# The first feed-forward product of a two-layer encoder: one matmul for high and low tokens in four of seven products

## The chip, the core and the metric

The kernel runs on one NeuronCore of a Trainium2 chip. The metric is the time of one execution on the device, in microseconds (us); several runs are made and their median is given.

TensorE (PE in the profile) multiplies and writes its sums to PSUM, a memory of eight banks with 512 columns of 32 bits each. VectorE (DVE) and ScalarE (ACT) work on elements in SBUF and PSUM. GpSimd (POOL) here mainly issues transfers that add to what lies at their target; SyncE (SP) issues plain transfers. Each engine goes through its own queue in order and waits for the others by semaphores.

## What is computed

Two layers, 512 tokens of width 1024. Each layer has attention of two kinds, and then the feed-forward part that this change touches:

```python
h = rmsnorm(x, mlp_norm[l])
u = jnp.square(jax.nn.relu(jnp.einsum('bsd,df->bsf', h, w_ff1[l])))
x = x + jnp.einsum('bsf,fd->bsd', u, w_ff2[l])
```

`w_ff1` is 1024 x 4096, `w_ff2` 4096 x 1024. All is float32.

## The kernel before, in words

**Precision by parts.** Each factor is split into a high part (rounded to the matmul's own format, fp32r) and a low part (what is left). A product a·b is then three matmuls: high·high, high·low, low·high (`three`, L295). Weights come by DMA as float32 tiles of 128 x 1024 and are split on their way: ScalarE makes the high part `whi` (L131), VectorE the low part `wlo` (L132).

**Seven products for eight.** Both feed-forward products use a Strassen-Winograd scheme: the operands are cut into 2 x 2 blocks, and seven products of sums of blocks replace eight. For the first product, the sums of token blocks lie in `T_hi`, `T_lo` (`opening`, L884, makes them, number 0 to 3), the plain tokens in `h_hi`, `h_lo`. The sums of weights are made on the fly. With W11, W12, W21, W22 as the four blocks, the tile called y holds W11, z holds W12, x holds W21 and has W22 added by a second transfer on GpSimd's queue (L852), w holds W22.

**Groups and units.** A layer's 4096 columns go in 4 groups (g = 0 to 3). In a group come the 14 units of the first product (seven products q in the order of `HALVES` L50, each for two halves c of the columns), then the seven forms of the second product (`FORMS` L43: 11, 21, x1, 22, x2, x3, x4), with 24 matmuls of 512 columns each. A unit (q,c) has 24 matmuls of 256 columns: two blocks of columns i, four steps cc along the width, three matmuls each (L1121 to L1124). Its moving operand is a block of 256 tokens (`MOVES`, L945), its stationary one a piece of the weights.

**What happens with the sums.** Products share PSUM banks: bank a takes product 1, then 6, 7 and 4 on top of it; bank c takes 2; bank b takes 5 and then 3. In between `tap` (L960) reads the running sums: product 1's sum is copied to F1 by ScalarE (L970), 2 is added to F1 by VectorE (L972); after 6 the sum is copied to F0 (L975); after 7 to F2 (L977) with bank b added (L978); after 3 bank b is added to F0 (L983); after 4 the sum goes straight from PSUM. Each of F0 to F3 is then bent: ReLU and square, two passes of ScalarE (L967). Some combinations of F0 to F4 follow on VectorE (`behind_3`, L999; `behind_4`, L1007), and `roll` splits an F into high and low parts `Ah`, `Al` for the second product (L245).

**What sets the order.** The order on each engine is that in which the program issues, kept by `line` (L267), which chains all splits, taps, bends, rolls and gathers on ScalarE and on VectorE. When a unit is issued, `W.next` (L162) first issues the weight splits up to four units ahead (`do_split`, L147); then the deferred bends and rolls of the unit before (`come_to`), then the unit's matmuls, then its tap. There are five pairs of tiles for split weights, so the split four units ahead can only run when the unit before the current one is done. So at unit (1,0) of a group, the splits up to the fifth unit of `HALVES` stand ahead of the tap of (1,0), on both engines.

**Hooks.** `then` (L907 ff.) hangs work behind a split: behind the split of 5, `sum1` "y" (L862) adds W11 to x on VectorE, giving product 6's weights, and has W21 added to y by a GpSimd transfer (L864), giving product 7's; behind the split of 6 (in the first group of 7), `sum1` "z" adds W12, giving product 3's. The tiles for the next group are loaded behind splits of the second product: x behind those of form x4. `paced` makes such a load wait for the last split. The first group's tiles are loaded during attention.

```python
def do_split(self, n, ahead=None):
    while self.split < min(n, self.stop):
        ...
        self.split_part(i, 0, 1024)
        ...
        for fn in self.then.pop(i, ()):
            fn()
```

## Time and profile before

| | us |
|---|---|
| median of 3 runs | 1120.12 (1119.45 to 1121.89) |
| the profiled execution | 1119.62 |
| its span in the profile | 1117.8 |
| first product, one group (third group of the first layer, 398.33 to 438.64) | 40.31 |
| second product, one group (438.64 to 476.75) | 38.11 |
| in the first of these, busy: VectorE, ScalarE | 31.71, 26.49 |

A line of the timeline reads: start in us from the span's start, duration in us, engine, line, operation, `out<-in` by the program's names, shapes, count; in brackets the idle time of the engine before it and what ended it. The tile names `q`, `yw`, `ww` and `cs` stand for raw weights, `f` for the first product's sums. A group's line (`x64 | 24.9, 390`) gives count, busy time in us and mean in ns.

### The profile page before, as it was taken

How to read it: one execution, taken by the hardware profiler on the slowest of the kernel's cores; microseconds unless marked ns; L12 is line 12 of the kernel's file. 1: busy time of each engine (PE TensorE's matmuls, PEld its weight loads, DVE VectorE, ACT ScalarE, POOL GpSimd, SP SyncE). 2: the span in 40 equal slices, each digit the busy share in tenths (PEclk: the TensorE clock that was granted, in tenths of full speed). 3: DMA queues.
4: the chain of work that ended last, by engine and by line, in shares of the span. 5: the costliest groups of instructions: out<-in, count | busy, mean ns of one | idle time of the engine just before them, and what ended most of it. 6: DMA issues, size and time to landing. Idle time of an engine off the chain costs nothing.

```text
span 1117.8 us, 17696 instructions
## 1 busy us (share of the span) xinstructions
PE 1109.3 (99%) x6654; PEld 985.1 (88%) x6654; DVE 929.5 (83%) x1230; ACT 709.5 (63%) x1113; POOL 176.9 (16%) x257
## 2 busy tenths in 40 slices
PE   9999999999999999999999999999999999999997
PEld 7888989889889899899888889888998998998986
DVE  7878789788897877878888787897988888888787
ACT  6546666677767557567555467675777665565675
POOL 1001334210210110201000014440101102011022
PEclk9999999999999999999999999999999999999999
DMA  7746334266887776876537463523578768859665
GB/s 249 208 123 203 114 116 114 81 170 188 186 197 214 167 176 204 189 190 158 123 113 208 119 177 113 157 77 142 105 229 185 189 189 187 206 138 202 172 135 148
DMA packets 60613, 183.37 MB, mean 164 GB/s; under 512 B 7536, under 2 KB 8816, under 8 KB 60528
## 3 DMA queue, kind: packets, MB, share of 16 engines
q1 hardware_dynamic: 46416, 131.62, 37.1%
q0 software_dynamic: 13824, 50.34, 25.7%
q8 instruction: 53, 0.87, 0.3%
q10 hardware_dynamic: 288, 0.28, 0.1%
q14 instruction: 32, 0.26, 0.1%
HBM read 154.95 MB, written 2.10 MB: 140 GB/s over the span
## 4 chain that ended last, share of the span: by engine, by line
PE 85%; DVE 5%; DMA 4%; issue 3%; ACT 2%; POOL 1%; POOLq 0%; DVEq 0%; SPq 0%; ACTq 0%
PE f L300 8%; PE f L298 8%; PE f L299 8%; DMA q<-in_w 3%; PE x L299 2%; PE x L298 2%; PE x L300 2%; PE wo L298 2%; PE wo L299 2%; PE wo L300 2%; DVE wlo L132 1%; DMA st1d1q<-hl1d1k 1%; PE T1s L623 1%; PE T0s L623 1%; PE v0u L298 1%
## 5 line engine op out<-in xcount | busy, mean ns | idle before, releaser
L132 DVE TENSOR_TENSOR wlo<-q,whi 128x1024 fp32r<-128x1024 f32 x184 | 223.6, 1220 | 23.9 <-ACT whi L131 22.6
L131 ACT ACTIVATE whi<-q 128x1024 fp32r<-128x1024 f32 x184 | 191.2, 1052 | 65.3 <-DMA q<-in_w 32.3
L298 PE MATMUL f<-T_hi,whi 128*128 128x256 f32 x512 | 145.5, 284 | 0.0
L300 PE MATMUL f<-T_hi,wlo 128*128 128x256 f32 x512 | 144.9, 283 | 0.0
L299 PE MATMUL f<-T_lo,whi 128*128 128x256 f32 x512 | 144.9, 283 | 0.0
L876 POOL DMA_DIRECT2D q<-in_w x64 | 56.2, 913 | 366.2 <-DVE wlo L132 346.4
L298 PE MATMUL f<-h_hi,whi 128*128 128x256 f32 x384 | 108.8, 283 | 0.0
L299 PE MATMUL f<-h_lo,whi 128*128 128x256 f32 x384 | 108.7, 283 | 0.0
L300 PE MATMUL f<-h_hi,wlo 128*128 128x256 f32 x384 | 108.7, 283 | 0.0
L299 PEld LDWEIGHTS f<-T_lo,whi 128*128 128x128 f32 x512 | 98.3, 192 | 0.0
L298 PEld LDWEIGHTS f<-T_hi,whi 128*128 128x128 f32 x512 | 98.3, 192 | 0.0
L300 PEld LDWEIGHTS f<-T_hi,wlo 128*128 128x128 f32 x512 | 98.2, 192 | 0.0
L967 ACT ACTIVATE F<-F 128x512 f32<-128x512 f32 x112 | 70.4, 629 | 21.7 <-DVE F L972 17.8
L131 ACT ACTIVATE whi<-raw 128x1024 fp32r<-128x1024 f32 (+1 forms) x58 | 55.7, 970 | 31.7 <-PE wo L299 6.9
L298 PEld LDWEIGHTS f<-h_hi,whi 128*128 128x128 f32 x384 | 73.7, 192 | 0.4
L299 PEld LDWEIGHTS f<-h_lo,whi 128*128 128x128 f32 x384 | 73.7, 192 | 0.3
L300 PEld LDWEIGHTS f<-h_hi,wlo 128*128 128x128 f32 x384 | 73.7, 192 | 0.1
L132 DVE TENSOR_TENSOR wlo<-raw,whi 128x1024 fp32r<-128x1024 f32 (+1 forms) x58 | 68.1, 1186 | 5.7 <-ACT whi L131 5.7
L245 ACT ACTIVATE Ahx<-F 128x1024 fp32r<-128x1024 f32 x32 | 34.0, 1061 | 52.1 <-PE x L299 24.4
L245 DVE TENSOR_TENSOR Alx<-F,Ahx 128x1024 fp32r<-128x1024 f32 x32 | 39.2, 1225 | 8.6 <-ACT Ahx L245 8.6
L245 DVE TENSOR_TENSOR Al<-F,Ah 128x1024 fp32r<-128x1024 f32 x24 | 29.4, 1224 | 18.0 <-ACT Ah L245 18.0
L556 POOL TENSOR_TENSOR sig1s<-sig1s,C1s 128x128 f32<-128x128 f32 (+3 forms) x32 | 28.5, 892 | 57.6 <-DVE C1s L553 46.7
(994 smaller groups left out, 3242.0 us busy)
## 6 DMA issues: line engine op xcount, KB each, us to landing
q<-in_w SPq DMA_DIRECT2D x100, 512.0 KB, 5.1
q<-in_w POOLq DMA_DIRECT2D x84, 512.0 KB, 7.0
raw<-in_w SPq DMA_DIRECT2D x62, 512.0 KB, 4.2
yw<-in_w SPq DMA_DIRECT2D x12, 512.0 KB, 4.5
yw<-in_w POOLq DMA_DIRECT2D x12, 512.0 KB, 5.6
cs<-in_w SPq DMA_DIRECT2D x8, 512.0 KB, 7.9
ww<-in_w SPq DMA_DIRECT2D x8, 512.0 KB, 4.0
x<-in_xT SPq DMA_DIRECT2D x8, 256.0 KB, 4.2
```

Of the source, the lines that this page charges most:

```text
L131: h = nc.scalar.activation(hi[:, a:b], raw[:, a:b], AF.Copy)
L132: self.last = h, nc.vector.tensor_tensor(out=lo[:, a:b], in0=raw[:, a:b], in1=hi[:, a:b].bitcast(F32), op=ALU.subtract)
L245: return nc.scalar.activation(hi, src, AF.Copy), nc.vector.tensor_tensor(out=lo, in0=src, in1=hi.bitcast(F32), op=ALU.subtract)
L298: return (nc.tensor.matmul(pt, ah, bh, start=first, stop=False, skip_group_check=onto), nc.tensor.matmul(pt, ah, bl, start=False, stop=Fal ...
L299: nc.tensor.matmul(pt, ah, bl, start=False, stop=False, skip_group_check=onto),
L300: nc.tensor.matmul(pt, al, bh, start=False, stop=last, skip_group_check=onto))
L556: nc.gpsimd.tensor_mul(sig[:, 0:wd], sig[:, 0:wd], C[:, 1 : wd + 1])
L623: nc.tensor.transpose(pt[:, n * P : (n + 1) * P], u["w"][qi][:, kb * P : (kb + 1) * P], ident)
L876: paced(nc.gpsimd.dma_start(t, quad(g, q, c), accum_op=ALU.add))
L967: nc.scalar.activation(o, o if i is None else i, fn, scale=by)))
```

## The change

1. The high and low parts of the tokens come to lie in one tile (`h2`, `T2`). In the products 1, 2, 6 and 4 one matmul of 512 columns takes the high weights against high and low tokens, and writes the two sums side by side: columns 0 to 255 of a bank hold high·high, 256 to 511 high·low. The matmul low·high has 256 columns as before and goes onto the first half. Products 5, 3 and 7 keep their three matmuls.
2. So bank a becomes four banks (0 to 3: two blocks of columns for each c). Sums are forked in PSUM: after product 1, ScalarE copies both banks of a into two others (c, banks 4 to 7), and product 2 accumulates on the copy; after product 6, ScalarE copies the low half of a into a bank b, and 5 and 3 accumulate on it. The taps add high and low halves when they take them, in pieces of 256 columns; after 4 the sum goes through F3 by a copy and an addition.
3. The order of the products becomes 1, 2, 6, 5, 3, 7, 4. Product 6's weights are made by `sum1` "y" ahead of the split of 6 (a new kind of hook, `first`), as W11 + x in the tile y; product 3's by `sum1` "z" in the tile z, behind the split of 6 (first group: behind the one of the next unit).
4. Product 7's weights can no longer be made in the tile y, so W11 is loaded anew and W21 added to it (`fill("7")`), behind the split of 6 and `sum1` "z". The load of form 21 moves behind the split of 5.
5. The roll of form 21 goes in two halves, one for each c; `opening` 1 is issued at (1,1) in place of (2,0), 3 at (7,0). The transposes for the MLP norm's sums move from behind (1,0) to behind (6,1) of the second group.

```diff
-HALVES = ("1", "2", "5", "6", "7", "3", "4")
-LAYS = (("5", 1), ("6", 0), ("6", 1), ("7", 0))
+HALVES = ("1", "2", "6", "5", "3", "7", "4")
+LAYS = (("5", 1), ("3", 0), ("7", 0), ("7", 1))
...
+            self.first.pop(i, lambda: None)()
             self.split_part(i, 0, 1024)
...
-    banks = {"t": 2, "mm": 2, "s": 3, "o": 1}
...
+    def one(k, name):
+        return ps.tile([P, 512], F32, tag=f"k{k}", name=name, bufs=1)
...
-    h_hi = cp.tile([P, KC, S], F32R, tag="h_hi", name="h_hi")
-    h_lo = cp.tile([P, KC, S], F32R, tag="h_lo", name="h_lo")
+    h2 = cp.tile([P, 2, KC, S], F32R, tag="h", name="h")
+    h_hi, h_lo = h2[:, 0, :, :], h2[:, 1, :, :]
...
-            T_hi = fr.tile([P, KC, S], F32R, tag="T_hi", name=f"T_hi{l}")
-            T_lo = fr.tile([P, KC, S], F32R, tag="T_lo", name=f"T_lo{l}")
+            T2 = fr.tile([P, 2, KC, S], F32R, tag="T", name=f"T{l}")
+            T_hi, T_lo = T2[:, 0, :, :], T2[:, 1, :, :]
...
             def fill(what, g, c):
-                t = homes[(what, c)] if what in "yw" else kept["x.z".index(what)][c]
-                for q in {"y": "1", "z": "2", "x": "5", "w": "4"}[what] + {"y": "7", "x": "63"}.get(what, ""):
+                if what == "7":
+                    t = homes["y", c] if g else (F[3], kept[1][0])[c]
+                else:
+                    t = homes[(what, c)] if what in "yw" else kept["x.z".index(what)][c]
+                for q in {"y": "16", "z": "23", "x": "5", "w": "4", "7": "7"}[what]:
                     W.raw[_AT[("q", l, g, q, c)]] = t
-                paced(nc.sync.dma_start(t, quad1(g, {"y": "11", "z": "12", "x": "21", "w": "22"}[what], c)))
-                if what == "x":
-                    nc.gpsimd.dma_start(t, quad1(g, "22", c), accum_op=ALU.add)
+                paced(nc.sync.dma_start(t, quad1(g, {"y": "11", "z": "12", "x": "21", "w": "22", "7": "11"}[what], c)))
+                if what in "x7":
+                    nc.gpsimd.dma_start(t, quad1(g, "22" if what == "x" else "21", c), accum_op=ALU.add)
...
             def sum1(what, g, c):
-                i = _AT[("q", l, g, "5", c)]
-                t, by = W.raw[i], W.raw[_AT[("q", l, g, "1" if what == "y" else "2", c)]]
+                t, by = (W.raw[_AT[("q", l, g, q, c)]] for q in ("65" if what == "y" else "36"))
                 line(v=nc.vector.tensor_add(t, t, by))
-                if what == "y":
-                    nc.gpsimd.dma_start(by, quad1(g, "21", c), accum_op=ALU.add)
...
-                    then("q", g, "5", c, sum1, "y", g, c)
-                    then("q", g, "6" if g else "7", c, sum1, "z", g, c)
-                    then("q", g, "2" if g else "7", c, fetch, g, "21", c)
+                    first("q", g, "6", c, sum1, "y", g, c)
+                    then("q", g, "6" if g or not c else "5", c if g else 1 - c, sum1, "z", g, c)
+                    if g:
+                        then("q", g, "6", c, fill, "7", g, c)
+                        then("q", g, "5", c, fetch, g, "21", c)
+                    else:
+                        then("q", g, "7", 1, fetch, g, "21", c)
+                        if c == 0:
+                            then("q", g, "6", 1, fill, "7", g, 1)
...
+            fill("7", 0, 0)
...
-                a, b = ((h_hi, h_lo), (T_hi, T_lo))[which]
-                return a[:, k + cc, t], b[:, k + cc, t]
+                m = (h2, T2)[which]
+                return m[:, 0, k + cc, t], m[:, 1, k + cc, t], m[:, :, k + cc, t]
...
+            def tap(g, q, c):
+                at = 512 * c
+                halves = [slice(at + 256 * i, at + 256 * i + 256) for i in range(2)]
+
+                def bend(n, scale=1.0):
+                    o = F[n][:, at : at + 512]
+                    for fn, by in ((AF.Relu, scale), (AF.Square, 1.0)):
+                        put_off.append(lambda fn=fn, by=by: line(nc.scalar.activation(o, o, fn, scale=by)))
+
+                def take(n, kind, lows):
+                    for h, t in zip(halves, sums[kind, c]):
+                        line(nc.scalar.copy(F[n][:, h], t[:, 256:512] if lows else t[:, 0:256]))
+
+                def more(n, kind, lows):
+                    for h, t in zip(halves, sums[kind, c]):
+                        line(v=nc.vector.tensor_add(F[n][:, h], F[n][:, h], t[:, 256:512] if lows else t[:, 0:256]))
 
                 if q == "1":
-                    line(nc.scalar.copy(f(1), pt))
+                    sums["c", c] = some((4 + 2 * c, 5 + 2 * c), f"fc{l}{g}{c}")
+                    for to, t in zip(sums["c", c], sums["a", c]):
+                        line(nc.scalar.copy(to, t))
                 elif q == "2":
-                    line(v=nc.vector.tensor_add(f(1), f(1), pt))
+                    take(1, "c", False)
+                    more(1, "c", True)
+                elif q == "6":
+                    take(0, "a", False)
+                    sums["b", c] = one(4 + c, f"fb{l}{g}{c}")
+                    for i, t in enumerate(sums["a", c]):
+                        line(nc.scalar.copy(sums["b", c][:, 256 * i : 256 * i + 256], t[:, 256:512]))
...
                     bend(1)
-                elif q == "6":
-                    line(nc.scalar.copy(f(0), pt))
+                elif q == "5":
+                    line(nc.scalar.copy(F[2][:, at : at + 512], sums["b", c]))
+                elif q == "3":
+                    o = F[0][:, at : at + 512]
+                    line(v=nc.vector.tensor_add(o, o, sums["b", c]))
+                    bend(0)
                 elif q == "7":
-                    line(nc.scalar.copy(f(2), pt))
-                    line(v=nc.vector.tensor_add(f(2), f(2), sums[("b", c)]))
+                    more(2, "a", False)
                     bend(2, -1.0)
                 elif q == "4":
-                    bend(3, -1.0, pt)
-                elif q == "3":
-                    line(v=nc.vector.tensor_add(f(0), f(0), pt))
-                    bend(0)
+                    take(3, "a", True)
+                    more(3, "a", False)
+                    bend(3, -1.0)
...
-                line(*roll("21"))
+                line(*roll("21", 512, 1024))
...
-                        n = {("2", 0): 1, ("5", 0): 2, ("3", 0): 3}.get((q, c))
+                        n = {("1", 1): 1, ("5", 0): 2, ("7", 0): 3}.get((q, c))
...
+                        if (q, c) == ("1", 0):
+                            for c_ in range(GP // 2):
+                                sums["a", c_] = some((2 * c_, 2 * c_ + 1), f"fa{l}{g}{c_}")
...
                         for i in range(2):
+                            joint, onto = q in "1264", q != "1"
+                            to = pt[:, 256 * i : 256 * i + 256] if spot == "b" else pt[i] if joint else pt[i][:, 0:256]
+                            steps = [[] for _ in range(2)]
                             for cc in range(4):
-                                ops = three(pt[:, 256 * i : 256 * i + 256], wpair(u, 4 * i + cc), mover(q, cc),
-                                            q in "125" and i == cc == 0, i == 1 and cc == 3, q not in "125")
-                                if i == cc == 0 and (q, c) != ("1", 0):
-                                    behind(ops[0], pe_end)
-                        pe_end = ops[2]
-                        tap(q, c, pt)
-                        if (g, q, c) == (1, "1", 0):
-                            ptr = bank("t", f"rs_m{l}")
+                                a, moved = wpair(u, 4 * i + cc), mover(q, cc)
+                                if joint:
+                                    steps[0].append((both_of(to), a[0], moved[2]))
+                                    steps[1].append((to[:, 0:256], a[1], moved[0]))
+                                else:
+                                    steps[0] += [(to, a[0], moved[0]), (to, a[0], moved[1]), (to, a[1], moved[0])]
+                            steps = steps[0] + steps[1] if q == "4" or not joint else [s_ for p_ in zip(*steps) for s_ in p_]
+                            for n_, s_ in enumerate(steps):
+                                op = nc.tensor.matmul(*s_, start=q == "1" and n_ == 0, stop=n_ == len(steps) - 1,
+                                                      skip_group_check=onto)
+                                if i == n_ == 0 and (q, c) != ("1", 0):
+                                    behind(op, pe_end)
+                        pe_end = op
+                        tap(g, q, c)
...
-                        if g == 0 and (q, c) == ("4", 0):
-                            put_off.append(lambda: behind_3(1))
+                        if (q, c) == ("4", 0):
+                            put_off.append(lambda: line(*roll("21", 0, 512)))
+                            if g == 0:
+                                put_off.append(lambda: behind_3(1))
...
-                                "27"[g == 0]: lambda: line(*roll("11")),
-                                "3": lambda: behind_3(0 if g == 0 else None),
+                                "53"[g == 0]: lambda: line(*roll("11")),
+                                "7": lambda: behind_3(0 if g == 0 else None),
                                 "4": lambda: behind_4(g == 0),
```

More of the change, by code (lines that the diff above doesn't have):

```diff
@@ L101, in __init__ @@
         self.loaded = self.split = self.used = self.turn = 0
-        self.raw, self.tiles, self.home, self.then, self.lows, self.came = {}, {}, {}, {}, {}, {}
+        self.raw, self.tiles, self.home, self.then, self.lows, self.came, self.first = {}, {}, {}, {}, {}, {}, {}
         self.depth = 3
@@ L184, in trunk, with some @@
     ps = ctx.enter_context(tc.tile_pool(name="ps", bufs=2, space=PSUM))
-    banks = {"t": 2, "mm": 2, "s": 3, "o": 1}
+    banks = {"t": (0, 1), "mm": (2, 3), "s": (4, 5, 6), "o": (7,)}
+    calls = dict.fromkeys(banks, 0)
+    def one(k, name):
+        return ps.tile([P, 512], F32, tag=f"k{k}", name=name, bufs=1)
+    def some(ks, name):
+        return [one(k, f"{name}{n}") for n, k in enumerate(ks)]
     turn = [0]
@@ L192, in bank @@
             turn[0] += 1
-        return ps.tile([P, 512], F32, tag=tag, name=name, bufs=banks[tag])
+        calls[tag] += 1
+        return one(banks[tag][calls[tag] % len(banks[tag])], name)
     if MAN:
@@ L986, in trunk, with roll @@
+                    bend(3, -1.0)
             rolled = {}
-            def roll(form):
-                nm = f"{form}{l}"
-                hi = rolls.tile([P, 1024], F32R, tag="Ah", name="Ah" + nm)
-                lo = rolls.tile([P, 1024], F32R, tag="Al", name="Al" + nm)
-                rolled[form] = hi, lo
-                return split(hi, lo, F[FSLOT[form]])
+            def roll(form, a=0, b=1024):
+                if a == 0:
+                    nm = f"{form}{l}"
+                    rolled[form] = [rolls.tile([P, 1024], F32R, tag=t, name=t + nm) for t in ("Ah", "Al")]
+                hi, lo = rolled[form]
+                return split(hi[:, a:b], lo[:, a:b], F[FSLOT[form]][:, a:b])
@@ L1030, in turned @@
             def turned(tb, j):
-                pt = bank("t", f"xT{tb}{j}")
+                pt = one(6 + (tb + j) % 2, f"xT{tb}{j}")
                 for k in range(4):
@@ L1131, in trunk @@
+                        pe_end = op
+                        tap(g, q, c)
+                        if (g, q, c) == (1, "6", 1):
+                            ptr = one(6, f"rs_m{l}")
                             for j in range(4):
@@ L1158, in trunk @@
                     if fresh_bank:
-                        chains[chain] = [bank(("s", "s", "s", "mm", "mm", "o")[2 * len(chains) + r], f"{form}{l}{g}{r}")
-                                         for r in range(2)]
+                        k = (6, 4, 0)[len(chains)]
+                        chains[chain] = some((k, k + 1), f"{form}{l}{g}")
                     to = chains[chain]
```

26 lines of the change are left out of this document (10 added, 16 removed).

## The prediction

> **What bounds the kernel now.** I read the page, then the waits of TensorE, then its timeline.
>
> ```profile
> span 1117.8 us, 17696 instructions
> PE 1109.3 (99%) x6654; PEld 985.1 (88%) x6654; DVE 929.5 (83%) x1230; ACT 709.5 (63%) x1113; POOL 176.9 (16%) x257
> PEclk9999999999999999999999999999999999999999
> ```
> ```profile
> PE wo L298 <- ACT vdh L245: 0.2, 1, 0.2
> PE 11001_3231 L298 <- DVE Y L1025: 0.2, 1, 0.2
> ```
>
> TensorE has work all the time, at full clock, and after its start it waits twice, 0.2 us each. So the time is the sum of TensorE's steps: a step taken away is gain, and any wait that is added is loss, one for one. A busy TensorE doesn't say how long a matmul holds it, since the matmuls overlap. That is read from the starts, in the timeline.
>
> ```profile
> 399.76 0.28 PE L298 MATMUL f<-h_hi,whi 128*128 128x256 f32 x1
> ...
> 409.72 0.28 PE L300 MATMUL f<-h_hi,wlo 128*128 128x256 f32 x1
> 225.00 0.39 PE L298 MATMUL wo<-vdh,whi 128*128 128x512 f32 x1
> ...
> 232.48 0.39 PE L298 MATMUL wo<-vdh,whi 128*128 128x512 f32 x1
> 316.40 0.39 PE L300 MATMUL 11000_3230<-whi,Alx 128*128 128x512 f32 x1
> 316.63 0.28 PE L298 MATMUL f<-h_hi,whi 128*128 128x256 f32 x1
> ```
>
> From 399.76 to 409.72 there are 83 steps of 256 columns: 0.120 us each. From 225.00 to 232.48 there are 33 steps of 512 columns: 0.227 us. A 512 step in front of a 256 one takes 0.23 as well. So two 256 steps cost 0.240, one 512 step 0.227: about 13 ns is a fixed price per matmul.
>
> **The matmuls (gain).** A product's unit (q,c) now has 24 steps of 256, 2.88 us. A joined unit has 8 steps of 512 and 8 of 256: 8 x 0.347 = 2.78 us. Joined are 4 of 7 products, 2 halves c, 4 groups, 2 layers: 64 units x 8 = 512 pairs, each 13 ns shorter: 6.7 us gained. That a 512 step keeps its 0.227 when its moving operand and its target lie in two pieces of 256 is not in these rows. If it took twice 0.120 the gain would be 0, and more than 6.7 would need a price below that of any 512 row. I take 6.7, by the rows of the same shape.
>
> [...]
>
> **The start of a group (loss).** Before, the first unit's sums were copied to SBUF and nobody on TensorE waited for it. Now ScalarE copies them into other banks, and (2,0) accumulates on that copy: TensorE waits for ScalarE one unit later. What is queued ahead of the copy? The weight splits are issued four units ahead, in a fixed order: the split of the fifth unit stands in ScalarE's queue before the copy. Group 3 of the first layer shows it.
>
> ```profile
> 476.75 0.28 PE L298 MATMUL f<-h_hi,whi 128*128 128x256 f32 x1
> 480.27 1.06 ACT L131 ACTIVATE whi<-q 128x1024 fp32r<-128x1024 f32 x1 [3.57 <-DMA q<-in_w]
> 481.85 0.57 ACT L970 COPY F<-f 128x512 f32<-128x512 f32 x1
> 483.78 1.06 ACT L131 ACTIVATE whi<-q 128x1024 fp32r<-128x1024 f32 x1 [1.36 <-DMA q<-in_w]
> 484.74 0.57 ACT L970 COPY F<-f 128x512 f32<-128x512 f32 x1
> 481.37 1.23 DVE L132 TENSOR_TENSOR wlo<-q,whi 128x1024 fp32r<-128x1024 f32 x1 [1.46 <-ACT whi L131]
> 482.63 1.22 DVE L862 TENSOR_TENSOR q<-q,yw 128x1024 f32<-128x1024 f32 x1
> 486.13 1.23 DVE L862 TENSOR_TENSOR q<-q,yw 128x1024 f32<-128x1024 f32 x1
> 487.27 1.22 DVE L132 TENSOR_TENSOR wlo<-q,whi 128x1024 fp32r<-128x1024 f32 x1
> ```
>
> The group starts at T = 476.75. The split of its fifth unit waits 3.57 us for the transfer that adds weights 22 to 21 (tile x) and begins at s = T + 3.52; the copy of the first unit comes only at 481.85, though (1,0) ended at 479.6. That was harmless. In the new order the fifth unit is (6,0), whose weights are 11 + x: at s only VectorE's addition can start, then the split. Step by step from s, with the spacings of these rows: addition 1.23 (sum y, c=0), split at s+1.26, its copy behind it at +0.97, done +0.58: (2,0) can go at about s+2.9 = T+6.4, where its turn is T+5.55: 0.9 late. For c=1 the order on VectorE is wlo(6,0) at s+2.36 (1.10 after its whi), sum z c=0 at s+3.62 (1.26 later), sum y c=1 at s+4.76 (1.14 later), done s+5.99; whi(6,1) s+6.02; the copy of (1,1) at s+6.98 (0.96 later), done s+7.57. With 0.1 for the signal (2,1) starts at s+7.67 = T+11.2, its turn being T + 3 x 2.78 = T+8.3. So by (2,1) TensorE has lost s - T - 0.65: 2.9 us here. The second x tile is there at 483.78 at the latest, before VectorE comes to it at 485.0, and doesn't decide.
>
> ```profile
> 398.33 0.28 PE L298 MATMUL f<-h_hi,whi 128*128 128x256 f32 x1
> 401.36 1.06 ACT L131 ACTIVATE whi<-q 128x1024 fp32r<-128x1024 f32 x1 [3.13 <-PE f L300]
> 322.35 0.60 PE L1132 MATMUL rs_m<-edge,ssq 128*128 128x128 f32 x4
> 323.88 1.06 ACT L131 ACTIVATE whi<-q 128x1024 fp32r<-128x1024 f32 x1 [1.47 <-DVE wlo L132]
> ```
>
> Six groups (1 to 3 of each layer) are so. The earliest s is T+3.03 (group 2 of the first layer), the latest T+4.41 (group 1, whose first unit ends at 322.35, so T counts as 319.47); the mean of the six is 3.6. Loss: 6 x (3.6 - 0.65) = 17.7 us.
>
> In the first group of a layer x lies ready, but the difference of tokens that product 6 needs moves from behind (1,1) to ahead of its splits.
>
> ```profile
> 239.96 0.28 PE L298 MATMUL f<-h_hi,whi 128*128 128x256 f32 x1
> 247.39 1.22 DVE L890 SCALAR_TENSOR_TENSOR hx0mdl<-hx0mdl,hx0mdh 128x1024 f32<-128x1024 f32 x1
> 248.64 1.06 ACT L245 ACTIVATE T_hi<-hx0mdl 128x1024 fp32r<-128x1024 f32 x1 [2.14 <-DVE hx0mdl L890]
> 249.74 1.23 DVE L245 TENSOR_TENSOR T_lo<-hx0mdl,T_hi 128x1024 fp32r<-128x1024 f32 x1 [1.12 <-ACT T_hi L245]
> ```
>
> VectorE came to it at 247.39, after a split and an addition for c=1 (2.4 us) that now stand behind it. I estimate 245.5, half a microsecond later than that subtraction gives, since the split of (6,0) now waits for its addition. Then T_hi 1.25 later, T_lo 1.10, sum y c=1 1.14, whi 1.26, copy 0.96, its end and the signal 0.67: 251.9. The turn of (2,1) is 239.96 + 8.3. Loss 3.6, two layers 7.2 us.
>
> **The end of a group (loss).** F3, which the second product's form 21 needs, was taken out of PSUM by ScalarE alone. Now each half of (4,c) is copied, added on VectorE, bent and rolled by halves, and VectorE's additions for c=0 stand behind the three subtractions that follow the last sum before 4.
>
> ```profile
> 354.46 0.28 PE L298 MATMUL f<-T_hi,whi 128*128 128x256 f32 x1
> 359.34 1.23 DVE L996 SCALAR_TENSOR_TENSOR F<-F,F 128x1024 f32<-128x1024 f32 x1
> 362.81 1.23 DVE L245 TENSOR_TENSOR Al<-F,Ah 128x1024 fp32r<-128x1024 f32 x1 [1.11 <-ACT Ah L245]
> 367.90 1.22 DVE L132 TENSOR_TENSOR wlo<-q,whi 128x1024 fp32r<-128x1024 f32 x1
> 371.13 0.39 PE L298 MATMUL x<-whi,Ahx 128*128 128x512 f32 x1
> ```
> ```profile
> L550 ACT ACTIVATE keep0s<-S0s 128x256 f32<-128x256 f32 x8 | 3.1, 384 | 1.7 <-PE S0s L536 1.7
> L132 DVE TENSOR_TENSOR wlo<-raw,whi 128x256 fp32r<-128x256 f32 x8 | 3.1, 418 | 0.3 <-ACT whi L131 0.3
> L967 ACT ACTIVATE F<-F 128x512 f32<-128x512 f32 x112 | 70.4, 629 | 21.7 <-DVE F L972 17.8
> ```
>
> Let E be the start of (4,0), 354.46 here. The third subtraction starts at E+4.88, VectorE is free at E+6.02. Two additions of 256 columns (0.42 each, 0.33 apart) end at 6.77; two bends of 0.63 at 8.1; half a roll, between the rows of 256 and 1024 columns 0.61 on ScalarE and 0.69 on VectorE, at 9.4. The additions for c=1 queue behind it, end at 10.1; bends 11.4; Ah 12.0; Al 12.7. Before, Al ended at E+9.58. Behind Al stand, as before, a subtraction, two additions to Y, the next roll and the split of the first weights of form x1 (367.90, ending at E+14.66). Al is 3.1 later, half of a full Al (0.45) is saved behind it: that split ends at about E+17.35. The second matmul of x1 wants it at 371.13 + 0.23 = E+16.90, now 0.2 earlier. Late by 0.75 with the signal, and the next weight's split by another 0.3 in the same way: about 1.0 us. Such a margin of 2.2 us is worked out from spacings, so bounds are 0 and 2 us. In the first groups one subtraction precedes instead of three and another follows; I take the same. Eight groups: 8 us.
>
> **What costs nothing, and what covers it.** Copies and additions in PSUM themselves: VectorE and ScalarE had idle time in a group; only the two places above are on the path. A copy from PSUM into PSUM stands in no row; the nearest is the 0.57 copy to SBUF, and I take that, with bounds 0.4 to 0.9 (worth 12 x 0.3 us). The extra loading of weights 11 for product 7, with its addition:
>
> ```profile
> q<-in_w SPq DMA_DIRECT2D x100, 512.0 KB, 5.1
> q<-in_w POOLq DMA_DIRECT2D x84, 512.0 KB, 7.0
> ```
>
> It starts after sum z (about T+8.5, c=1 T+13), on SP's queue ahead of the loads of form 21, then on GpSimd's, and lands 12 us later: T+20.5 and T+25. The split of (7,1) is then up to 2 us behind its place, and (5,1)'s copy in ScalarE's queue behind it, for which (3,1) waits at T+28: covered by about 1 us. Uncovered it costs what it is late: up to 2 us in six groups.
>
> **Sum.** The profiled execution took 1119.62 us (span 1117.8), 0.5 under the median of 1120.12. 1119.6 - 6.7 + 17.7 + 7.2 + 8 = 1145.8.
>
> **Rivals.**
> (a) Only the starts lose; the ends are covered because VectorE finds the 2.2 us somewhere: 1137.8.
> (b) The starts don't lose and the change is faster: if the transfer into x landed before s = T + 0.65, all splits would be done in time, TensorE would find each copy ready, and the time would be 1112.9. For it: TensorE waits nowhere today. Against it: the transfer lands at T+3 or later in all six groups, and the chain before it hangs on TensorE's own pace, so it won't come earlier.
> (c) Starts almost covered, gain and ends cancel: about 1120.
> (d) Worse: the load for product 7 is late (up to 12), or the 512 steps gain nothing (1152.5), or both: 1148 to 1162. [...]
>
> **How the numbers follow.** A measurement of this kernel tells 0.2% (2.2 us) from no change. Forecast 0.58, (a) 0.16, (b) 0.08, (c) 0.05, (d) 0.13. Faster 0.08, same 0.05, slower 0.87. The forecast's own bounds: starts by the 0.5 us that I don't know per group (4), ends 0 to 16, copies 4: 1134 to 1156. The range takes in (a) with its bounds and the nearer part of (d): 1130 to 1157.
>
> **What would show it.** In the profile after: joined units with 0.347 us per pair of starts; waits of TensorE on lines f, released by ScalarE's copies, near 0.9 us at (2,0) and 2 at (2,1) in six groups, 3.6 in the first ones; waits of form x1 on wlo near 0.7 and 0.3. TensorE's busy share falls below 98%. If TensorE still waits nowhere, the prediction is wrong and the time is near 1113; if it waits at the starts but not at x1, (a) holds.

## The result, and the profile after

| | before | after |
|---|---|---|
| median, us | 1120.32 (4 runs) | 1168.91 (4 runs, 1167.63 to 1172.56) |
| span of the profiled execution, us | 1117.8 | 1166.6 |
| TensorE, mean granted clock | 0.999 | 0.995 |

The changed kernel is slower by 4.4%: ratio 1.0437, 95% interval 1.0411 to 1.0464. The forecast of 1145.8 had the sign and about half of the size; 1168.9 lies outside its range of 1130 to 1157. (In the changed kernel's lines the feed-forward matmuls stand at L1174, the copies into other banks at L1002 and L1010, the copy of (5,c) at L1013, the second product's matmuls at L307 to L309, and the loads of weights at L862 and L864.)

The page's first lines for the changed kernel:

```profile
span 1166.6 us, 16950 instructions
PE 1123.1 (96%) x6142; PEld 959.0 (82%) x6142; DVE 937.3 (80%) x1302; ACT 745.0 (64%) x1249; POOL 177.9 (15%) x257
```

512 matmuls fewer, as the diff says, and TensorE is busy 96% where it was 99%: 43.5 us of its span have no work (8.5 before). The waits of TensorE by what they waited for (us in total, times, longest):

```profile
PE fb L1174 <- ACT F L1013: 12.0, 5, 2.9
PE fc L1174 <- ACT fc L1002: 11.1, 13, 2.0
PE x L308 <- DVE wlo L132: 5.3, 8, 1.6
PE 21130_10885 L307 <- ACT Ah L254: 1.4, 1, 1.4
```

Two of the forecast's waits are there: `fc` for ScalarE's copy at the start of a group, and `x` (form x1) for a low half. The largest row was forecast at nothing: `fb` waits for the copy of (5,1) at L1013. That is (3,1), which the forecast had "covered by about 1 us".

**The start of a group.** The timeline of the third group of the first layer, which starts at T = 411.37:

```profile
411.37 0.39 PE L1174 MATMUL fa<-h,whi 128*128 128x512 f32 x1
415.73 1.23 DVE L873 TENSOR_TENSOR yw<-yw,q 128x1024 f32<-128x1024 f32 x1 [1.19 <-DMA q<-in_w]
417.07 1.06 ACT L131 ACTIVATE whi<-yw 128x1024 fp32r<-128x1024 f32 x1 [5.79 <-DVE yw L873]
418.03 1.06 ACT L1002 COPY fc<-fa 128x512 f32<-128x512 f32 x2
418.66 0.50 PE L1174 MATMUL fc<-h,whi 128*128 128x512 f32 x1 [1.49 <-ACT fc L1002]
421.54 0.39 PE L1174 MATMUL fa<-T,whi 128*128 128x512 f32 x1
422.81 0.28 PE L1174 MATMUL fa<-T,wlo 128*128 128x256 f32 x1
423.34 0.50 PE L1174 MATMUL fc<-h,whi 128*128 128x512 f32 x1 [0.25 <-ACT fc L1002]
```

The chain is the one that was forecast: x lands, the sum on VectorE (415.73), the split (417.07), behind it in ScalarE's queue the copy that was due since (1,0) ended, and (2,0) waits 1.5 us for the first of the copy's two halves. But at 421.54, where (2,1) should stand and wait, TensorE does four pairs of product 6 (`fa<-T`) and only then (2,1): the order that the program was given puts half of (6,0) first, and 1.4 us of the wait is filled.

**The middle of a group.** The same group, from the reload of W11 for product 7's second half on:

```profile
425.26 0.33 SPq L862 DMA_DIRECT2D yw<-in_w  x1
431.94 0.88 POOL L864 DMA_DIRECT2D yw<-in_w  x1 [6.55 <-DMA yw<-in_w]
439.92 1.06 ACT L131 ACTIVATE whi<-yw 128x1024 fp32r<-128x1024 f32 x1 [4.81 <-DMA yw<-in_w]
440.89 0.57 ACT L1013 COPY F<-fb 128x512 f32<-128x512 f32 x1
438.90 0.28 PE L1174 MATMUL fb<-h,wlo 128*128 128x256 f32 x1
441.50 0.80 PE L1174 MATMUL fb<-h,whi 128*128 128x256 f32 x2 [2.33 <-ACT F L1013]
442.10 0.41 PE L1174 MATMUL fb<-h,wlo 128*128 128x256 f32 x1
442.31 0.63 PE L1174 MATMUL fb<-h,whi 128*128 128x256 f32 x2
```

W11 is issued at T+13.9; GpSimd issues the addition of W21 6.7 us later, when W11 has landed; that lands at T+28.5, 14.6 us after the first issue. ScalarE has waited 4.81 us by then, with the copy of (5,1) queued behind the split, and TensorE waits for the copy from 439.0 to 441.5.

**A half clock behind the wait.** The matmuls after 441.50 are 0.21 us apart for 256 columns (442.10 and 442.31 above) instead of 0.12. Stretches of the trace (length; busy time, with the count of instructions, of PE, PEld, DVE, ACT and POOL; granted clock; DMA share; GB/s):

```profile
355.80:359.20 3.40, 3.40 (x18) 3.40 (x18) 3.19 (x4) 2.39 (x3) 0.00 (x0) 0.51 0.54 183
441.00:444.60 3.60, 3.10 (x14) 3.10 (x15) 3.38 (x3) 3.30 (x4) 0.00 (x0) 0.53 0.40 135
528.50:532.00 3.50, 3.50 (x31) 3.50 (x30) 3.29 (x5) 2.37 (x3) 0.00 (x0) 1.00 0.64 179
```

Behind the waits at (3,1) of the second and third group the clock is halved for 3.4 us; behind the one of the fourth group (3.1 us long, the longest) it isn't. There is a third such stretch at 912.2, behind a start (0.50 from 912.3 to 915.6). Each loses 1.5 us: 3.4 us hold 16 steps of 0.213, which take 1.9 us at 0.120.

**Where the 48.8 us of span went.** From the starts of TensorE's steps in the two traces:

| | worked out as | us |
|---|---|---|
| joined matmuls | 8 groups x 0.47 (shown with the unjoined run below) | -3.8 |
| first groups of the layers | both products: 76.67 to 81.86, 76.35 to 81.01, and the 2 x 0.47 that they should have gained | +10.8 |
| starts, six later groups | (2,0) 1.54, 1.64, 1.56, 2.12, 1.05, 0.77; (2,1) 0.33, 0.41, 0.34, 0, 0.34, 0.69 | +10.8 |
| (3,1), five of these groups | 2.88, 2.49, 3.05, 2.28, 2.10 | +12.8 |
| half clock | 3 x 1.5 | +4.5 |
| second product, six later groups | 2.04, 2.15, 1.8, 1.73, 1.79, 3.2 longer than before | +12.7 |
| sum | | +47.8 |

### The profile page after: what moved, and what is told of

Same layout as the page of the kernel before. It is cut to its first block, busy times and chain, and to the rows that moved or that the text cites. A ratio compares the mean times of both kernels' runs of the same rounds, so it can differ in the third digit from the quotient of the medians.

```text
span 1166.6 us, 16950 instructions
## 1 busy us (share of the span) xinstructions
PE 1123.1 (96%) x6142; PEld 959.0 (82%) x6142; DVE 937.3 (80%) x1302; ACT 745.0 (64%) x1249; POOL 177.9 (15%) x257
## 4 chain that ended last, share of the span: by engine, by line
PE 45%; DVE 16%; DMA 15%; issue 13%; ACT 9%; POOL 1%; SPq 0%; DVEq 0%; POOLq 0%; ACTq 0%
DMA q<-in_w 9%; DMA yw<-in_w 5%; DVE wlo L132 5%; ACT whi L131 3%; ACT F L989 2%; PE x L308 2%; PE fb L1174 2%; PE x L309 2%; PE x L307 1%; DVE F L997 1%; PE wo L307 1%; PE wo L308 1%; PE wo L309 1%; DVE yw L873 1%; PE fa L1174 1%
## 5 line engine op out<-in xcount | busy, mean ns | idle before, releaser
L1174 PE MATMUL fa<-T,whi 128*128 128x512 f32 (+1 forms) x512 | 127.7, 340 | 1.1 <-DVE T L254 1.1
L132 DVE TENSOR_TENSOR wlo<-yw,whi 128x1024 fp32r<-128x1024 f32 x36 | 44.1, 1224 | 64.6 <-ACT whi L131 62.5
L1174 PEld LDWEIGHTS fa<-T,whi 128*128 128x128 f32 x512 | 86.1, 190 | 10.3 <-DVE T L254 1.8
L1174 PE MATMUL fa<-T,wlo 128*128 128x256 f32 x384 | 92.6, 282 | 0.7 <-DVE wlo L132 0.7
L1174 PEld LDWEIGHTS fa<-T,wlo 128*128 128x128 f32 x384 | 68.4, 190 | 3.9 <-DVE wlo L132 1.1
L1174 PE MATMUL fb<-h,whi 128*128 128x256 f32 x256 | 50.1, 297 | 12.0 <-ACT F L1013 12.0
L1174 PE MATMUL fc<-h,whi 128*128 128x512 f32 x128 | 48.4, 416 | 11.1 <-ACT fc L1002 11.1
L1174 PEld LDWEIGHTS fb<-h,whi 128*128 128x128 f32 x256 | 42.2, 203 | 13.1 <-ACT F L1013 13.0
L1174 PE MATMUL fb<-T,whi 128*128 128x256 f32 x256 | 46.5, 284 | 0.0
L1174 PE MATMUL fa<-h,whi 128*128 128x512 f32 x128 | 45.6, 398 | 0.0
L864 POOL DMA_DIRECT2D q<-in_w x18 | 16.1, 915 | 173.2 <-DMA q<-in_w 152.9
L1174 PEld LDWEIGHTS fc<-h,whi 128*128 128x128 f32 x128 | 24.7, 193 | 20.7 <-ACT fc L1002 15.3
```

The lines of the kernel that those rows point to most:

```text
L132: self.last = h, nc.vector.tensor_tensor(out=lo[:, a:b], in0=raw[:, a:b], in1=hi[:, a:b].bitcast(F32), op=ALU.subtract)
L864: nc.gpsimd.dma_start(t, quad1(g, "22" if what == "x" else "21", c), accum_op=ALU.add)
L1174: op = nc.tensor.matmul(*s_, start=q == "1" and n_ == 0, stop=n_ == len(steps) - 1, skip_group_check=onto)
```

## The experiments

The theory at first: each of these rows is a wait by itself, and goes when what it waits for is taken away. The rival: something else makes the kernel longer, and the waits only show it.

**Splits one unit later.**

```diff
-                        u = W.next("q")
+                        u = W.next("q", 1)
```

> In the first product a unit issues weight splits only up to three units ahead instead of four, so each split stands in the queues behind the tap of the unit before, not ahead of it. Theory (the copies in PSUM wait in ScalarE's queue behind a split whose weights are late): the waits of (2,0) and (2,1) in six groups (11 us) go, those of the first groups lose about 2 of 4 us, the waits of (3,1) (13 us) and the half-clock stretches after them (5 us) go, the waits in the second product stay: 1138 us, 1134 to 1143. Rival (the weights themselves come too late for their unit, wherever the split stands): 1166 to 1170. Second rival (the copy from PSUM into PSUM is slow): waits of (2,0) stay, 1150 or more.

Measured: 1170.88 us (4 runs), ratio 1.0455 (1.0437 to 1.0472). The forecast of 1138 fell; the time is 0.9 above the range of the first rival, late weights. Its waits:

```profile
PE fa L1174 <- DVE F L997: 7.3, 3, 2.8
PE x L307 <- ACT whi L131: 4.2, 5, 1.6
PE fa L1174 <- ACT whi L131: 4.1, 2, 2.5
PE fb L1174 <- ACT F L1013: 2.3, 2, 1.9
```

The row of `fc` is gone altogether, and that of `fb` is down from 12.0 to 2.3. In their place stand waits for the splits themselves (`whi`), which now come too late everywhere, in the second product's first forms too, and for VectorE's additions at L997. So the copies did stand behind the splits; but moving all splits only exchanges the waits, and the run can't say what the starts are worth.

**x without block 22** (in groups 1 to 3).

```diff
-                if what in "x7":
+                if what == "7" or what == "x" and g == 0:
```

> In groups 1 to 3 the addition of block 22 to tile x is left out (products 3, 5 and 6 then have weights without that block), so x is there about 7 us sooner; all else as in the changed kernel. Theory (the start waits for x): (2,0) and (2,1) no longer wait in six groups, one half-clock stretch less, (3,1) and the second product wait as before: 1156 us, 1152 to 1161. Rival (the copies in PSUM or the longer taps are what (2,0) waits for): 1166 to 1170.

Measured: 1167.59 us (2 runs), in the rival's range. The waits:

```profile
PE fb L1174 <- ACT F L1013: 13.4, 6, 3.0
PE fc L1174 <- ACT fc L1002: 7.0, 14, 1.4
```

`fc` fell by 4.1 and `fb` rose by 1.4, in six groups now instead of five. I took the two waits to be in series on one chain in absolute time (x, sum, split of 6, reload, addition of 21, split of (7,1), copy): what the start gains, (3,1) partly waits away again. This run fits that and does not show it.

**Product 7 without block 21** (in groups 1 to 3).

```diff
-                if what in "x7":
+                if what == "x" or what == "7" and g == 0:
```

> In groups 1 to 3 the addition of block 21 to the newly loaded block 11 is left out (product 7 then has the weights of block 11 alone), so its weights are there 7 to 8 us sooner. Theory (the new load is late, its split blocks ScalarE's queue, and (3,1) waits for the copy behind it): the waits of (3,1) (13 us) and two or three half-clock stretches (3 to 5 us) go, the starts and the second product wait as before: 1152 us, 1148 to 1157. Rival (ScalarE is behind because of the many pieces of 256 columns): 1166 to 1170.

Measured: 1150.08 us (2 runs), ratio 1.0266. As expected. The row `fb` is gone, the others stand:

```profile
PE fc L1174 <- ACT fc L1002: 11.0, 11, 2.4
PE x L308 <- DVE wlo L132: 4.9, 8, 1.6
```

18.8 us, more than the 12.8 of the waits at (3,1). The half-clock stretches don't explain the rest: this run has three as well (mean clock 0.995, as in the changed kernel), now behind longer waits at the starts. Most of it lies in the second product: over the six later groups it is 4.7 us shorter than in the changed kernel, so a part of what the table puts down to the ends seems to go with product 7's late weights. That cause isn't shown: in the run with product 7 by subtraction, below, these weights aren't late either, and its second products are as long as in the changed kernel.

**Subtractions at the end of the group, earlier.** VectorE's second subtraction goes behind the tap of (4,0), the third behind that of (4,1), so that the additions onto F3 no longer queue behind them.

```diff
                         tap(g, q, c)
+                        if (q, c) == ("4", 0):
+                            line(v=nc.vector.tensor_sub(F[0], F[1], F[0]))
+                        elif (q, c) == ("4", 1):
+                            less(1, 4, 1)
...
-                                "7": lambda: behind_3(0 if g == 0 else None),
-                                "4": lambda: behind_4(g == 0),
+                                "7": lambda: behind_3(0),
+                                "4": lambda: behind_4(),
```

> Of the three subtractions that follow product 7's sum, only the first stays where it is; the second is issued behind the tap of (4,0), the third behind the tap of (4,1), in all groups. Nothing is left out. Theory (the additions for F3 stand behind the subtractions on VectorE, and what follows in the second product is late by that): the waits in the second product fall from 16 us to about 4, the rest stays: 1157 us, 1153 to 1162. Rival (the added work of VectorE itself, not its order, makes the second product late): 1165 to 1170.

Measured: 1157.16 us (1156.76 to 1158.14), ratio 1.0330 (1.0315 to 1.0345). As expected. In its waits form x1 has 0.6 us once instead of 5.3 in eight:

```profile
PE x L308 <- DVE wlo L132: 0.6, 1, 0.6
```

And the second product of the third group is back at the 38.11 us of before: 11.8 us, nearly the whole row of the table, and it is VectorE's queue.

**Both loads plain.** Both of the edits to the loads together.

> Leaves out, in groups 1 to 3 of both layers, the two additions of a weight block that are made on the way in (block 22 onto x, block 21 onto the new load for product 7); the weights of products 6, 5, 3 and 7 there are therefore not the right sums, the instructions are all the others. Theory now: the wait at (2,0)/(2,1) and the wait at (3,1) hang on one chain in series (x lands, sum, split of (6,0), reload of 11, adding 21, split of (7,1), copy of (5,1)), which runs in absolute time: to shorten only its first part moves the start earlier but lets (3,1) wait the longer, so that taking out block 22 alone brought 1.3 us. With its second part gone too, the first part must pay: the start waits of the groups 1 to 3 (some 11 us in the run with plain product 7) fall to 0.4 each as in the run with plain x, and the time goes from 1150.1 to 1141 (1138 to 1145). Rival: the start waits cost nothing, because what they hold back is made up by a later wait in any case (the end of the group, FF2's first form): 1148 to 1151.

Measured: 1147.3 us (1147.04 to 1147.56, 2 runs), 2.8 below the run with product 7 alone and not the 9 of the theory. The starts do pay in the traces: over the six later groups the first products together are 7.2 us shorter (4.5 less of waits at (2,0), and the three stretches of half clock are gone: mean clock 0.999). But the second products are 2.2 longer, with three waits of 0.8 at form x4 for a low half, and the very first group is 1.5 longer. So the number fell, and later waits took back a good part, as the rival has it; whether the waits hang on one chain in series is not settled by this run. `fc` still has 7.0 us: with x there in time, (2,0) waits 1.54 in the second group of each layer, to the same hundredth in both layers, and 0.36 in the others. A wait that keeps its length when the transfer changes is not the transfer's.

**Product 7 by subtraction.** With W11 + W21 = (W11 + W21 + W22) - W22, the weights can be made from what product 6 and product 4 hold, with no load at all.

```diff
-                        then("q", g, "6", c, fill, "7", g, c)
+                        then("q", g, "6", c, minus, g, c)
...
+            def minus(g, c):
+                t = W.raw[_AT[("q", l, g, "7", c)]] = homes["y", c]
+                line(v=nc.vector.tensor_sub(t, t, W.raw[_AT[("q", l, g, "4", c)]]))
```

> Computes everything: in groups 1 to 3 product 7's weights W11+W21 are not loaded anew and added to in transit, but made by VectorE in place from the sum that product 6 has just used, less block 22 that product 4 holds (one subtraction of 128x1024 for each of 12 tiles, 1.23 us each in the row of the sums). Theory: the late load was the whole matter behind the waits at (3,1), so this comes out where the run without block 21 did, or up to 2 us above it, the 12 subtractions lying beside the matmuls: 1151 (1148 to 1154). Rival: VectorE, busy 80% of the span already, passes the delay on (the low halves of the splits and the additions onto copies come later by 1.2 us a tile), and a good part of the gain goes: 1156 to 1165.

Measured: 1156.23 us (1155.03 to 1159.26), ratio 1.0318 (1.0299 to 1.0337): 12.7 under the changed kernel, but 6.2 over the run without block 21, at the rival's near end.

```profile
PE fc L1178 <- ACT fc L1006: 17.3, 14, 2.3
```

(L1178 and L1006 are the former L1174 and L1002.) The (3,1) wait is gone and `fc` has 6.3 us more: the subtraction for c=0 stands on VectorE ahead of the sum for (6,1), so the split of (6,1) and the copy of (1,1) come later by its 1.2 us. Again the queue.

**Subtraction and ends together.**

> Computes everything: the subtraction for product 7 and the earlier subtractions at the group's end together. Theory: the two losses lie in different stretches (the middle of a group's first product, and its second product) and add: 1168.9 less 17.8 less 11.7 = 1139.4 (1136 to 1143). Rival: they share VectorE, and the three subtractions moved up delay the additions at the end of the group: 1144 to 1152.

Measured: 1142.66 us (1141.15 to 1144.17, 2 runs). Compared with the run just before 13.6 us, no less than the 11.8 of the ends alone: the two losses add. `fc` with 17.0 us is what is left.

**x early too.** From the second group on x is loaded far ahead into w's tiles, and the second opening is moved.

```diff
-                        then("f", g, "11", c, fill, "w", g + 1, c)
+                        then("f", g, "21" if g else "11", c, fill, "x", g + 1, c)
...
-                        then("f", g, "x4", c, fill, "x", g + 1, c)
+                        then("f", g, "x2", c, onto_x, g + 1, c)
+                        then("f", g, "x3", c, fill, "w", g + 1, c)
...
-                        n = {("1", 1): 1, ("5", 0): 2, ("7", 0): 3}.get((q, c))
+                        n = {("2", 0): 1, ("5", 0): 2, ("7", 0): 3}.get((q, c))
```

> Computes everything. On top of the run before: from group 1 on, x is loaded into the tiles that held w while the second product of the group before is still at its second form (x2 for adding block 22), w goes where x3 was, block 21 of the second product where x was; and in the first groups the second opening is put before (2,0) instead of (1,1). Theory: with x there in time, no start of groups 1 to 3 waits (11 us of waits gone), and the first groups lose half of their 4 to 5 us: 1139.4 - 11 - 4 = 1124 (1120 to 1130), that is still just behind the kernel before, since the shorter matmul steps bring only 5.1 us and the copies and additions around the forked sums keep the rest. Rival: the start waits are not x's but the queue of ScalarE's, three splits and copies of two sums in the time of one product: 1133 to 1140. Second rival: all waits go, and the kernel comes out ahead of the one before: 1113 to 1118.

Other than the expectation says, one part isn't computed: in the last group of each layer the load of the tables goes onto the tile that by then holds half of block 21 for the second product's form 21. The order and the number of the instructions are as meant. Measured: 1161.39 us (1158.84 to 1167.70), 18.7 slower than the run with subtraction and ends. Its third group of the first layer starts at 415.72:

```profile
416.52 2.35 DVE L132 TENSOR_TENSOR wlo<-q,whi 128x1024 fp32r<-128x1024 f32 x2
418.79 1.22 DVE L879 TENSOR_TENSOR yw<-yw,ww 128x1024 f32<-128x1024 f32 x1
420.13 1.06 ACT L131 ACTIVATE whi<-yw 128x1024 fp32r<-128x1024 f32 x1 [4.51 <-PE fa L1185]
421.09 1.06 ACT L1013 COPY fc<-fa 128x512 f32<-128x512 f32 x2
```

No transfer is waited for any more (the bracket at 420.13 names TensorE; what came last was the sum, which ends at 420.01), and the copy still starts at T+5.4, because the chain in front of it is full: two low halves on VectorE, the sum, the split on ScalarE, then the copy. x's landing had hidden this floor. (2,0) waits 0.36 here and 1.54 in the second groups, as in the run with both loads plain, and (2,1) 1.6 in all six groups. Altogether the starts wait 2.8 us less than in the run with subtraction and ends. What makes this run slower (22.5 us between the two profiled executions) is new waits at form x4 for its split weights, 16.5 us in the starts of TensorE's steps, and stretches of half clock of 20.5 us in all (mean clock 0.989), about 9 of loss by the 1.5 for each 3.4 of the changed kernel; the rearranged loads are the likely cause, but no run took them back one by one.

**Copies first.** On the run with subtraction and ends: during product 1 the splits come one unit later, and the subtraction for product 7 goes behind the split of 3.

```diff
-                        u = W.next("q")
+                        u = W.next("q", q == "1")
...
-                        then("q", g, "6", c, minus, g, c)
+                        then("q", g, "3", c, minus, g, c)
```

> Computes everything. The run with subtraction and ends, and two moves more: during product 1 alone the splits are issued one unit later, so that ScalarE's copies of product 1's sums stand ahead of the splits of (6,0) and (6,1) on its queue instead of behind them; and the subtraction for product 7 is issued behind the split of product 3's weights instead of (6,c)'s, out of VectorE's way. Theory: the start waits come from the queues and not from x's landing (with x there in time the waits of 1.54 and 1.59 stood unchanged): the copy waits behind a split, the split behind VectorE's sum, the sum behind two low halves and the last addition of the group before. With the copies in front they are gone: 1142.7 less the 19.2 us of waits at (2,0) and (2,1) that the run before has, of which some 2 come back at (6,0): 1125.5 (1121 to 1131). Rival: the splits now late are the bound instead, (6,0) waits for its low half as long as (2,0) did: 1138 to 1146.

Measured: 1132.25 us (1131.47 to 1132.57), ratio 1.0097 (1.0080 to 1.0114): 10.4 gained where 17 were expected. In the trace there is no `fc` row left in the six later groups, and two of them take 39.9 us for the first product (45.8 and 43.6 in the changed kernel). What is missing is in the first groups, which got longer by 3.4 and 2.5 us (both products 83.3 and 81.6, from 80.0 and 79.1; a stretch of half clock in each, 1.5 us, is part of it):

```profile
PE fa L1178 <- ACT whi L131: 4.5, 2, 2.9
PE fa L1178 <- DVE wlo L132: 1.5, 2, 0.8
```

There x was never late, and later splits only come late.

**Unjoined.** The same with every 512-column matmul split in two again.

> Computes everything; the run just before with each 512-column matmul of the four products split into two 256-column ones again (same sums, same copies, same order otherwise): 512 pairs of 0.233 and 0.117 us become 512 triples of 0.120. Theory: the joint matmul is worth the 10 ns a pair that the trace of the changed kernel shows, 5.1 us: 1130.6 where the run before is at 1125.5 (a difference of 4 to 7). Rival one: the 13 ns a pair of the prediction, 6.7 us and more. Rival two: nothing (under 1.5 us), the steps being hidden in the waits.

Measured: 1133.14 us (1131.22 to 1133.85), ratio 1.0105 (1.0090 to 1.0120): between the medians 0.9 us, which the two intervals don't tell apart and which would fit the second rival, nothing. The traces tell them apart, in a group without any wait. Unjoined, first matmul of the first product and first of the second:

```profile
405.65 0.40 PE L1180 MATMUL fa<-h,whi 128*128 128x256 f32 x2
...
445.96 0.40 PE L307 MATMUL 11020_4811<-whi,Ah 128*128 128x512 f32 x1
```

and joined, the same two in the next run below:

```profile
403.57 0.39 PE L1178 MATMUL fa<-h,whi 128*128 128x512 f32 x1
...
443.41 0.40 PE L307 MATMUL 11020_4619<-whi,Ah 128*128 128x512 f32 x1
```

40.31 us (as before the change) against 39.84: 0.47 us a group, 7.3 ns for each of 64 pairs, 3.8 us over eight groups, where 5.1 were expected. In such a group the step from a 512-column matmul to the 256-column one behind it has a mean of 0.236, the other one 0.117 us. That the medians show only 0.9 of the 3.8 has two places in the traces: the joined run has one stretch of half clock more (1.5), and waits 3.1 and 1.7 us at the first groups' (6,0) where the unjoined one waits 1.9 and 1.6.

**Copies first, in the later groups alone.**

```diff
-                        u = W.next("q", q == "1")
+                        u = W.next("q", g > 0 and q == "1")
```

> Computes everything; as the run with copies first, but the splits of product 1 are put behind the copies in groups 1 to 3 alone, and the first groups keep the order of the run with subtraction and ends. Theory: in the first groups the later splits cost 3.4 and 2.5 us (83.3 and 81.6 us for the two products where the run with subtraction and ends has 80.0 and 79.1), in the later groups the copies ahead brought all of the gain: 1132.3 - 5.9 = 1126.4 (1124 to 1129). Rival: the first groups' loss is taken back by the groups behind them, whose start is then earlier against the same loads: 1130 to 1133.

Measured: 1125.43 us (1123.81 to 1127.07), ratio 1.0048 (1.0033 to 1.0063). As expected. The longest of its waits behind the start of the kernel:

```profile
PE fc L1178 <- ACT fc L1006: 2.1, 2, 1.1
PE fa L1178 <- DVE T L254: 1.3, 2, 1.1
```

Both are the first groups', twice each.

**First groups too.**

```diff
+                        if g == 0 and (q, c) == ("2", 0):
+                            opened(1)
-                        u = W.next("q", g > 0 and q == "1")
+                        u = W.next("q", q == "1" and (g > 0 or c > 0))
```

(`opened(1)` is the split of the second opening, taken out of `opening(1)`.)

> Computes everything; as the run just before, and in the first groups the second opening is cut in two: its addition on VectorE stays ahead of (1,1), its split goes behind the copies of (1,1), and the split of (6,1) behind that. Theory: of the 2.9 us at (6,0) and (2,1) of each first group most goes: 1126.4 - 5 = 1121.4 (1118 to 1125), level with the kernel before (1120.6): with every wait that the change made taken out, its 512 pairs bring 3 us at most (0.4 us a group between the joined and the unjoined run), and half a microsecond of order is left in the first groups. Rival: the first groups' openings, four on VectorE and ScalarE within one product, cannot be put anywhere without a wait while product 6 stands before product 5: 1125 to 1129.

Measured: 1124.44 us (5 runs, 1122.82 to 1125.32), ratio 1.0039 (1.0027 to 1.0052). Between theory and rival, and not to be told from the run before: the waits at (2,1) and (6,0) went, and waits of up to 1.0 us before product 7 took their place. The first groups are 3.8 and 2.7 us longer than before the change, the six others together level or a little shorter (0.8 us less in all, the last group of each layer by its first product alone). No version that I found beats the kernel before; why the first groups keep 6.5 us stays open. The trace names the places:

```profile
PE fa L1185 <- DVE wlo L132: 1.5, 2, 0.8
PE 11000_3196 L307 <- ACT Ah L254: 0.8, 1, 0.8
```

In each first group TensorE loses 1.0 us at product 7 to a wait for a low half, 1.0 at form 11 to one for `Ah`, and 0.4 to 0.8 ahead of products 5 and 7 (counted in the starts of its steps, a little more than the waits themselves). The wait at form 11 stands in the changed kernel too and not in the kernel before, and no run took it away.

## Why the prediction was wrong

- **The bound: right.** TensorE's steps set the time and every added wait is paid one for one, and 1.5 us more behind the three where the clock fell.
- **The step that failed** is the one under "What costs nothing": the new load for product 7, "covered by about 1 us. Uncovered it costs what it is late: up to 2 us in six groups", entered in the sum with 0. It measured 12.8 us of waits. The two transfers took 14.6 us where the sum of two medians, 5.1 and 7.0, gave 12; they were issued 0.9 later than reckoned; so they landed 3.5 later than forecast (T+28.5 for T+25), and that ate the 1 us of cover and left waits of 2.1 to 3.1. That ScalarE's copy, which (3,1) needs, is queued behind the split was forecast rightly. With the load replaced by a subtraction, and with the block left out, these waits went. Rival (d) had this late load with "up to 12"; it was named and given 0.13, and its range, 1148 to 1162, was still too low, as the other terms were larger too.
- **The ends: mechanism right, size off.** 8 us forecast, 12.7 in the six later groups alone; x1's second matmul waits 0.5 in six groups (0.75 forecast) and 1.75 in the first ones. Ahead of it, at form 21, four groups wait 0.3 to 1.6 for `Ah`, and behind it, at form x4, two wait 0.7 and 0.8 for a low half; the forecast had neither. Moving two subtractions brought 11.8, so VectorE's queue was the place, as forecast.
- **The starts: place right, size too large, cause only in part.** 17.7 forecast, 10.8 measured; (2,0) waits 0.8 to 2.1 where 0.9 was forecast, (2,1) 0 to 0.7 where it was 2. In the group shown x let the sum start at T+4.36, where the forecast had T+3.03 for that group; by its formula the loss would be 4.36 - 0.65 = 3.7 us. But the order has half of (6,0) ahead of (2,1), 1.4 us of work for the wait; 1.64 + 0.41 + 1.4 = 3.45 is near it. What fell too is the cause: the forecast had the loss end when x lands in time (rival b), and took x to land at T+3 or later in all six groups, though two of its rows (323.88 and 401.36) name VectorE and TensorE as what ended the wait, and no transfer. Two runs with x there in time show a floor by the queues of VectorE and ScalarE alone; the loss went only when the copies were put ahead of the splits.
- **The first groups:** 7.2 forecast and 2 for their ends; 10.8 measured. The sum is near by luck. (2,1) waits 1.2 in each where 3.6 was forecast; x1 waits 1.75 for 1.0; the rest are waits that the forecast didn't have, 1.0 and 0.5 at (6,0), 0.5 at product 7's low half and 1.0 at form 11 for `Ah`.
- **The matmuls:** 6.7 forecast, 3.8 measured. A matmul with 512 columns behind a 256 one and in two pieces takes 0.236, not the 0.227 of the rows that I took (and the 256 one behind it 0.117). The pair came out 7.3 ns shorter (0.47 us for 64), where I had 13.
- **The clock:** the forecast's sum has no term for it, and the kernel before shows no such stretch (granted clock 1.00 up to 1115 us). Three stretches of half clock cost 4.5 us behind waits of 2.1 to 2.9, 1.5 us each.
- **The bounds:** 4, 8 and 4 us either way, as the forecast gives them, add to 1130 to 1162, more than the 1134 to 1156 that it states. 1168.9 lies outside both.

By size the miss is 1168.9 - 1145.8 = 23.1 us: (3,1) +12.8, clock +4.5, ends of the six later groups +6.7, first groups with their ends +1.6, matmuls +2.9, starts -6.9, which comes to 21.6.

## What to carry to other kernels

When a copy on another engine becomes an input of the engine that bounds the kernel, write down everything that stands ahead of it in that engine's queue, and what that waits for in turn; data that come early don't help a copy that is queued late (with x there in time, (2,0) still waited 0.36 to 1.54 us). A chain of two transfers whose sum of medians leaves 1 us of cover can be uncovered, as here with 14.6 us for 12: give it a price and not a zero. And a gain of some nanoseconds per matmul is worth less than one wait of 2 us in each group: here all joined matmuls together bring 3.8 us, less than the 4.5 that the clock alone took back.

## What the hardware showed besides

In the feed-forward parts of nine of the fourteen traces the clock was halved, each time during a wait of TensorE or within 2 us behind it, for 3.4 us or twice that; the longest of these waits was 3.6 us. In the changed kernel the granted clock fell to 0.50 at 355.8, 441.2 and 912.2; the waits ended at 355.39, 441.50 and 911.38. The shortest such wait without another long one beside it was 1.7 us (the run with copies first), and the wait of 3.05 us that began at 525.0 in the changed kernel had none behind it (granted clock 1.00 from 528.5 to 532.0). What sets these waits apart is not shown: no run varied one of them for that.

A ScalarE copy of 512 columns from PSUM into PSUM, for which no row of the trace before stood, takes what a copy to SBUF takes: in the changed kernel the copies onto `fc` have a mean of 0.564 us, those from `fb` to SBUF 0.568, and two in a row take 1.06.
